# Other distances between moving rows and weights in four feed-forwards, and a later switch to normalized x in one

## The chip, the cores and the metric

The kernel runs on one core of a Trainium2 chip. The metric is device time in microseconds: the median of three timed runs. One further execution was taken with the hardware profiler; all views below are of that one.

## What is computed

Two blocks follow one another on 256 rows of 1024 columns, all in float32. The first block (reference `first_block`) has two layers. Each has a feed-forward, a mixer (a state-space scan in layer 0, pooling in layer 1) and a second feed-forward, each on a normalized and modulated input; layer 0 runs beside them a second stream, the context `h`. The second block is another mixer network; the change does not touch it.

```python
def swiglu(u, wg, wu, wd):
    return (jax.nn.silu(u @ wg) * (u @ wu)) @ wd
...
def modulate(x, g, shift, scale):
    return rmsnorm(x, g) * (1 + scale) + shift
...
        x = x + 0.5 * m[:, 8] * swiglu(modulate(x, norm_g[i, 2], m[:, 6], m[:, 7]),
                                       ffn_w_gate[i, 1], ffn_w_up[i, 1], ffn_w_down[i, 1])
```

Gate and up have 1024 x 2816 weights, down has 2816 x 1024. The modulation `m` is a product of `silu(c)` with `ada_w`.

## The kernel before

Everything is held transposed: columns on the 128 partitions, tokens along them, so x is 8 tiles of 128 x 256 (`xT`, `KD` = 8, `T` = 256). A product in float32 is made of three matmuls in float32r (`mm3`, L301 to L303): high weights by high rows, high weights by low rows, low weights by high rows. The weights stand still (128 x 128 a matmul), the rows move (256, 258 or 512 columns).

`Weights` streams all weights of the program in one order. `load` (L52) fetches a raw piece on SP's queue; `prepare` makes of 1024 columns the high part `whi` on ScalarE (L68) and the low part `wlo` on VectorE (L69), into rings of four buffers each, two units ahead of their use. A unit is one gate or up tile of eight 128 x 128 pieces, so 24 matmuls. A buffer of the ring is free once the unit four before has been used up.

There are four feed-forwards. The first in time is joint: latent and context rows together, 512 columns, in three parts, its intermediate in `hh0` and `hl0` (high and low). The other three are calls of `ffn` (L810), on the latent rows alone: the text calls them the first, second and third. Each goes over 22 tiles of the intermediate (`f`): gate into the bank `pg`, up into `pu`, SiLU, product, and a split into `hh` and `hl`; then eight down tiles of 66 matmuls each, into `po`.

The rows of the first five tiles (`FIRST`) are `xh` and `xl`, x scaled but without its reciprocal norm R and shift, with two columns more that hold the shift, so 258. Their results are scaled and shifted afterwards on VectorE and ScalarE (`shifted` L379, L828 to L833). Meanwhile `norm_mod` (L395) writes the normalized x into `xn` (high by ScalarE L398, low by VectorE L399, from a product at L397), two of its eight tiles after each of f = 1 to 4 (`EARLY`, L812, L839). From tile 5 on the rows are `xn`, 256 columns, and ScalarE and VectorE have one operation each in place of the six. From f = 2 on, the first and second feed-forward also make one modulation column a tile (`ada_column`, L236: 128 x 1024 on VectorE, its weights `adaraw` loaded on SP's queue). Five PSUM banks serve `pg`, `pu` and `po` in turn.

The order on each engine is set by a scheduling layer, from the order in which the program is written; engines work through it in order.

`lead` puts an unused tile of that many bytes ahead of `xn`, and so moves all tiles of the feed-forward. All buffers of `whi` and `wlo` start at 320 bytes modulo 512, and weight pieces step by 512 bytes, rows by 1024 or 2048. So within a stage the distance from weights to moving rows, modulo 512, is the same for all matmuls.

Of the kernel before, what the change touches and what calls it, by code (L numbers as in the profile page):

```python
# [10 lines left out]
F32 = mybir.dt.float32  # L11
F32R = mybir.dt.float32r
AF = mybir.ActivationFunctionType
# [4 lines left out]
P = 128  # L18
# [71 lines left out]
def build(ctx: ExitStack, tc, a, out):  # L90
# [22 lines left out]
    def nm(s):  # L113
        uid[0] += 1
        return f"{s}{uid[0]}"
# [173 lines left out]
    def half_cols(l, s, m):  # L289
        t = consts.tile([P, KD], F32, name=f"H{l}{s}{m}")  # L290
        V.tensor_scalar(t, mod(l, s, m), 0.5, None, op0=OP.mult)
        return t
# [514 lines left out]
                pass  # L807


    def ffn(R, nxt, H, tail, n_ada, late=None, lead=0):  # L810

        EARLY = ((), (0, 1), (2, 3), (4, 5), (6, 7))  # L812
        FIRST = len(EARLY)
        with tc.tile_pool(name=nm("ffn"), bufs=1) as fp:
            if lead:
                fp.tile([P, lead // 4], F32, name=nm("lead"))
            xn = [fp.tile([P, KD, T], F32R, name=nm("xn")) for _ in range(2)]
            hh = fp.tile([P, NF, T], F32R, name=nm("hh"))
            hl = fp.tile([P, NF, T], F32R, name=nm("hl"))
            for f in range(NF):  # L820
                pg, pu = bank("mm", nm("pg")), bank("mm", nm("pu"))

                (mh, ml), n = ((xh, xl), T + 2) if f < FIRST else (xn, T)
                dense_tile(pg[:, :n], W.next(), 0, KD, mh, ml, n)
                dense_tile(pu[:, :n], W.next(), 0, KD, mh, ml, n)
                tg = tmp.tile([P, T], F32, tag="t1k", name=nm("tg"), bufs=2)
                if f < FIRST:
                    tu = tmp.tile([P, T], F32, tag="t1k", name=nm("tu"), bufs=2)  # L828
                    shifted(pg, R, tg)
                    b = tmp.tile([P, 1], F32, tag="bg", name=nm("bg"), bufs=4)  # L830
                    V.tensor_copy(b, pu[:, T:T + 1])
                    V.tensor_mul(tu, pu[:, :T], R)
                    V.scalar_tensor_tensor(tu, tu, b, tg, op0=OP.add, op1=OP.mult)  # L833
                else:
                    tu = tg
                    S.activation(tg, pg[:, :T], AF.Silu)
                    V.tensor_mul(tu, pu[:, :T], tg)
                split(hh[:, f, :], hl[:, f, :], tu)
                for d in EARLY[f] if f < FIRST else ():  # L839
                    norm_mod(xn[0][:, d, :], xn[1][:, d, :], d, xT[:, d, :], R, nxt.A, nxt.B)  # L840
                if f == 2 and late:
                    late()
                if f > 1:
                    ada_do(n_ada)
            table()
            for d in range(KD):
                po = bank("mm", nm("po"))
                for f0, n in PARTS:
                    dense_tile(po[:, :T], W.next(), 0, n, hh, hl, T, f0, f0 == 0, f0 + n == NF)
                V.scalar_tensor_tensor(xT[:, d, :], po[:, :T], H[:, d:d + 1], xT[:, d, :],  # L850
                                       op0=OP.mult, op1=OP.add)
                tail(d)
# [76 lines left out]

    with l0_stack:  # L930
        with tc.tile_pool(name="ffn0", bufs=1) as fp:
            fp.tile([P, 32], F32, name="lead0")
            hh = fp.tile([P, 8, 2 * T], F32R, name="hh0")
            fp.tile([P, 40], F32, name="lead1")
            hl = fp.tile([P, 8, 2 * T], F32R, name="hl0")
            for f0, nf in PARTS:
                for f in range(nf):
                    pg, pu = bank("mm", nm("pg")), bank("mm", nm("pu"))
                    dense_tile(pg, W.next(), 0, KD, uh, ul, 2 * T)
                    dense_tile(pu, W.next(), 0, KD, uh, ul, 2 * T)  # L940
                    sg = fp.tile([P, 2 * T], F32, tag="sg", name=nm("sg"), bufs=2)
                    S.activation(sg, pg, AF.Silu)
                    V.tensor_mul(sg, sg, pu)
                    split(hh[:, f, :], hl[:, f, :], sg)
                    if f0 + f == 0:
                        for n, src in enumerate(("c", "c_ctx")):
                            cond_load(l0, n, a[src])
                            S.activation(csb[n], csb[n], AF.Silu)
                    ada_do(4)
                if f0 == 0:  # L950
                    ada_until(0, 2)
                    h2c, h2x = half_cols(0, 1, 2), half_cols(0, 0, 2)
                last = f0 + nf == NF
                if last:
                    ada_until(0, 4)
                    A1c, A1x = scale_cols(0, 1, 1, 4), scale_cols(0, 0, 1, 4)
                    B1c, B1x = mod(0, 1, 3), mod(0, 0, 3)
                    st2 = l0.tile([P, 2 * T], F32, name="st2")
                    shifts(B1x, T - 2)
                    table()  # L960
                for d in range(KD):
                    po = bank("mm", nm("po"))
                    dense_tile(po, W.next(), 0, nf, hh, hl, 2 * T)
                    V.scalar_tensor_tensor(xC[:, d, :], po[:, :T], h2c[:, d:d + 1], xC[:, d, :],
                                           op0=OP.mult, op1=OP.add)
                    V.scalar_tensor_tensor(xT[:, d, :], po[:, T:], h2x[:, d:d + 1], xT[:, d, :],
                                           op0=OP.mult, op1=OP.add)
                    if last:
                        sq = l0.tile([P, 2 * T], F32, tag="sq2", name=nm("sq2"), bufs=1) if d else st2
                        S.activation(sq[:, :T], xC[:, d, :], AF.Square)  # L970
                        S.activation(sq[:, T:], xT[:, d, :], AF.Square)
                        if d:
                            V.tensor_add(st2, st2, sq)
                        scaled(d, xT[:, d, :], A1x, T)
                    ada_do(3)
# [40 lines left out]
    with tc.tile_pool(name="ada1", bufs=1) as ap:  # L1016
        ada_state["pool"] = ap
        cond_load(ap, 0, a["c"])
        ada_stop(1, 8)
        ffn(R, nxt, H8, after_ffn1, 1, lambda: S.activation(csb[0], csb[0], AF.Silu), lead=320)  # L1020


        nxt = state["n"]
        R = nxt.st.rstd()

        def after_ffn2(d):
            if d == 0:
                state["n"] = Next(scale_cols(1, 0, 1, 4))
            state["n"](d)

        ffn(R, nxt, half_cols(1, 0, 2), after_ffn2, 1, lead=320)
        ada_until(1, 8)

    def pool_phase(pp, st, pmat, tail):
# [78 lines left out]
            state["n"] = Final()  # L1113
        state["n"](d)

    ffn(R, nxt, half_cols(1, 0, 8), after_ffn3, 0, lead=320)
    f = state["n"]

    def norm_first():
# [744 lines left out]
```

## Time and profile before

| | us |
|---|---|
| median of three timed runs | 1912.84 |
| the three runs | 1906.72, 1912.84, 1916.23 |
| the profiled execution | 1924.61 |
| its span | 1922.8 |
| mean granted clock of TensorE in it | 0.989 |

| stage | from | to |
|---|---|---|
| first feed-forward, tiles 0 to 4 | 726.84 | 757.83 |
| the same, tiles 5 to 21 | 757.83 | 862.18 |
| the same, down | 862.18 | 924.37 |
| second, tiles 0 to 4 | 924.37 | 954.09 |
| second, tiles 5 to 21 | 954.09 | 1050.70 |
| second, down | 1050.70 | 1112.88 |
| third, tiles 0 to 4 | 1128.59 | 1158.19 |
| third, tiles 5 to 21 | 1158.19 | 1251.57 |
| third, down | 1251.57 | 1311.41 |

The times of stages are starts of their first matmul in the profiled execution, from the start of its span. Matmuls overlap: one is listed with a duration of 276 ns or more, while the next starts after less than half of that. So a stage is read by its length and its number of matmuls, not by their durations. The granted clock is 1.00 at 2.4 GHz and 0.50 at 1.2 GHz.

### The profile page before, as it was taken

The page shows a single profiled execution, that of the slowest core. Times are in us where ns is not written, and L with a number is a line of the kernel's source. Part 1 is how long each engine was busy: PE and PEld are TensorE (multiplying, and loading weights), DVE is VectorE, ACT ScalarE, POOL GpSimd, SP SyncE. Part 2 cuts the span into 40 slices and gives each one's busy share as a digit, 9 for nine tenths or more (in the row PEclk, how much of TensorE's full clock was granted, in tenths as well). Part 3 has the DMA queues.
Part 4 walks back from the last instruction along what each step waited for, and adds up shares of the span by engine and source line. Part 5 has one row for each costly group of instructions (what it writes and reads, how often), then busy time and mean ns, then how long its engine had stood idle before and what let it go on. Part 6 is the DMA issues. An engine that isn't in the chain of part 4 may idle for free.

```text
span 1922.8 us, 37344 instructions
## 1 busy us (share of the span) xinstructions
PE 1869.3 (97%) x15576; PEld 1690.3 (88%) x15576; DVE 1425.4 (74%) x2539; ACT 1041.7 (54%) x1659; POOL 0.2 (0%) x4
## 2 busy tenths in 40 slices
PE   8999999998999999999999999999999999999998
PEld 3888888887767789999999999999998998999887
DVE  5898788777898799855755587566698765698764
ACT  5322222355778666544544455456556656756573
POOL 0000000000000000000000000000000000000000
PEclk9999999999999999999999999999999999999999
DMA  8767788633333437755555645556544254536232
GB/s 314 261 238 280 278 301 312 231 120 114 110 107 135 132 132 277 256 172 184 198 178 170 195 161 182 178 192 197 195 149 174 88 164 153 189 115 221 94 110 88
DMA packets 82441, 353.12 MB, mean 184 GB/s; under 512 B 12928, under 2 KB 31424, under 8 KB 51552
## 3 DMA queue, kind: packets, MB, share of 16 engines
q1 hardware_dynamic: 82272, 350.73, 52.5%
q8 instruction: 122, 2.00, 0.4%
q14 instruction: 47, 0.39, 0.1%
HBM read 348.80 MB, written 1.12 MB: 182 GB/s over the span
## 4 chain that ended last, share of the span: by engine, by line
PE 83%; ACT 6%; DVE 5%; DMA 3%; issue 2%; SPq 0%; DVEq 0%; ACTq 0%
PE po L301 6%; PE po L303 6%; PE po L302 6%; PE pg L301 5%; PE pg L302 5%; PE pg L303 5%; PE pu L302 5%; PE pu L303 5%; PE pu L301 5%; PE pfm L301 3%; PE pfm L302 3%; PE pfm L303 3%; ACT whi L68 2%; PE ptm L1202 1%; PE pw L302 1%
## 5 line engine op out<-in xcount | busy, mean ns | idle before, releaser
L68 ACT ACTIVATE whi<-wraw 128x1024 fp32r<-128x1024 f32 (+1 forms) x485 | 504.2, 1041 | 668.5 <-PE po L302 189.2
L69 DVE TENSOR_TENSOR wlo<-wraw,whi 128x1024 fp32r<-128x1024 f32 (+1 forms) x485 | 580.7, 1199 | 242.9 <-ACT whi L68 238.3
L301 PE MATMUL po<-hh,whi 128*128 128x256 f32 (+1 forms) x704 | 217.5, 309 | 0.0
L303 PE MATMUL po<-hh,wlo 128*128 128x256 f32 (+1 forms) x704 | 216.9, 308 | 0.0
L302 PE MATMUL po<-hl,whi 128*128 128x256 f32 (+1 forms) x704 | 216.6, 308 | 0.0
L236 DVE SCALAR_TENSOR_TENSOR adascr<-adaraw,csb 128x1024 f32<-128x1024 f32 x152 | 185.7, 1222 | 31.9 <-DMA adaraw<-in_ada 29.4
L301 PE MATMUL pfm<-xh,whi 128*128 128x256 f32 x640 | 190.2, 297 | 0.0
L302 PE MATMUL pfm<-xl,whi 128*128 128x256 f32 x640 | 182.4, 285 | 0.0
L303 PE MATMUL pfm<-xh,wlo 128*128 128x256 f32 x640 | 180.9, 283 | 0.0
L303 PEld LDWEIGHTS po<-hh,wlo 128*128 128x128 f32 x704 | 133.0, 189 | 8.2
L301 PEld LDWEIGHTS po<-hh,whi 128*128 128x128 f32 x704 | 132.9, 189 | 7.5
L302 PEld LDWEIGHTS po<-hl,whi 128*128 128x128 f32 x704 | 132.2, 188 | 7.8
L301 PEld LDWEIGHTS pfm<-xh,whi 128*128 128x128 f32 x640 | 122.8, 192 | 3.7 <-issue 1.4
L302 PEld LDWEIGHTS pfm<-xl,whi 128*128 128x128 f32 x640 | 122.6, 192 | 2.1 <-issue 1.4
L303 PEld LDWEIGHTS pfm<-xh,wlo 128*128 128x128 f32 x640 | 122.4, 191 | 1.2 <-issue 1.0
L301 PE MATMUL pg<-xn,whi 128*128 128x256 f32 x408 | 115.5, 283 | 2.8 <-ACT xn L398 1.6
L302 PE MATMUL pg<-xn,whi 128*128 128x256 f32 x408 | 115.5, 283 | 0.8 <-DVE xn L399 0.8
L301 PE MATMUL pu<-xn,whi 128*128 128x256 f32 x408 | 114.6, 281 | 0.7 <-ACT whi L68 0.7
L303 PE MATMUL pg<-xn,wlo 128*128 128x256 f32 x408 | 115.0, 282 | 0.0
L302 PE MATMUL pu<-xn,whi 128*128 128x256 f32 x408 | 114.6, 281 | 0.0
L303 PE MATMUL pu<-xn,wlo 128*128 128x256 f32 x408 | 114.5, 281 | 0.0
L301 PE MATMUL pg<-xh,whi 128*128 128x512 f32 (+1 forms) x296 | 104.1, 352 | 0.4 <-ACT xh L369 0.4
(468 smaller groups left out, 4814.7 us busy)
## 6 DMA issues: line engine op xcount, KB each, us to landing
wraw<-in_ffn_gu SPq DMA_DIRECT2D x88, 1024.0 KB, 5.0
adaraw<-in_ada SPq DMA_DIRECT2D x64, 1024.0 KB, 6.8
wraw<-in_w SPq DMA_DIRECT2D x60, 1024.0 KB, 5.0
wraw<-in_ffn_d SPq DMA_DIRECT2D x24, 960.0 KB, 4.8
wraw<-in_ssd_wi SPq DMA_DIRECT2D x20, 1024.0 KB, 5.1
wraw<-in_w_out SPq DMA_DIRECT2D x16, 1024.0 KB, 5.1
wraw<-in_ffn_d SPq DMA_DIRECT2D x24, 448.0 KB, 3.3
adan<-in_ada_n SPq DMA_DIRECT2D x8, 1024.0 KB, 8.3
```

The lines of the kernel that those rows point to most:

```text
L68: nc.scalar.activation(hi[:, :n], raw[:, o:o + n], AF.Copy)
L69: nc.vector.tensor_sub(lo[:, :n], raw[:, o:o + n], hi[:, :n].bitcast(F32))
L236: V.scalar_tensor_tensor(scr, t[:, h, :], 1.0, csb[s], op0=OP.mult, op1=OP.mult, accum_out=macc[l, s][:, n:n + 1])
L301: TE.matmul(o, wh, xh, start=start, stop=False)
L302: TE.matmul(o, wh, xl, start=False, stop=False)
L303: TE.matmul(o, wl, xh, start=False, stop=stop)
L1202: TE.matmul(o, h, wh[:, sl], start=k == 0, stop=False)
```

## The change

It changes two things. In the first feed-forward, `EARLY` writes one tile of `xn` after each of f = 1 to 8, so that `FIRST` is 9: tiles 5 to 8 use `xh` and `xl` with 258 columns too. And the unused tiles get other sizes, now with a second one between `xn` and `hh`, so that six distances change.

```diff
-    def ffn(R, nxt, H, tail, n_ada, late=None, lead=0):
-
-        EARLY = ((), (0, 1), (2, 3), (4, 5), (6, 7))
+    def ffn(R, nxt, H, tail, n_ada, late=None, lead=(0, 0), EARLY=((), (0, 1), (2, 3), (4, 5), (6, 7))):
...
-            if lead:
-                fp.tile([P, lead // 4], F32, name=nm("lead"))
+            if lead[0]:
+                fp.tile([P, lead[0] // 4], F32, name=nm("lead"))
             xn = [fp.tile([P, KD, T], F32R, name=nm("xn")) for _ in range(2)]
+            if lead[1]:
+                fp.tile([P, lead[1] // 4], F32, name=nm("lead"))
...
-            fp.tile([P, 32], F32, name="lead0")
+            fp.tile([P, 48], F32, name="lead0")
             hh = fp.tile([P, 8, 2 * T], F32R, name="hh0")
-            fp.tile([P, 40], F32, name="lead1")
+
...
-        ffn(R, nxt, H8, after_ffn1, 1, lambda: S.activation(csb[0], csb[0], AF.Silu), lead=320)
+        ffn(R, nxt, H8, after_ffn1, 1, lambda: S.activation(csb[0], csb[0], AF.Silu), lead=(192, 384),
+            EARLY=((),) + tuple((d,) for d in range(KD)))
...
-        ffn(R, nxt, half_cols(1, 0, 2), after_ffn2, 1, lead=320)
+        ffn(R, nxt, half_cols(1, 0, 2), after_ffn2, 1, lead=(160, 192))
...
-    ffn(R, nxt, half_cols(1, 0, 8), after_ffn3, 0, lead=320)
+    ffn(R, nxt, half_cols(1, 0, 8), after_ffn3, 0, lead=(224, 192))
```

As the two programs lay their tiles out, the distances from weights to moving rows, in bytes modulo 512:

| rows | before | after |
|---|---|---|
| joint, `hh0` and `hl0` | 0 and 160 | 64 and 64 |
| first, `xn` | 192 | 64 |
| first, `hh` and `hl` | 192 | 448 |
| second, `xn` | 192 | 32 |
| second, `hh` and `hl` | 192 | 224 |
| third, `xn` | 192 | 96 |
| third, `hh` and `hl` | 192 | 288 |

`xh` and `xl` stay at 192. The output projection before the first feed-forward, whose rows `gh` and `gl` stand at 128 and 384, is not changed.

The distances move no instruction; `EARLY` does. On VectorE, where the last rows of `xn` are written, the order before is (`adascr` is a modulation column, `nm` the product of x and R, `bg` a shift):

```order
L833 SCALAR_TENSOR_TENSOR tu_6950<-tu_6950,bg_6955,tg_6949 128x256
L377 TENSOR_TENSOR xl<-macc_89,xh 128x8x2
L397 SCALAR_TENSOR_TENSOR nm_6961<-xT,A_3048,rstd_6546 128x256
L308 TENSOR_TENSOR hl_6567<-tu_6950,hh_6566 128x256
L397 SCALAR_TENSOR_TENSOR nm_6965<-xT,A_3048,rstd_6546 128x256
L399 SCALAR_TENSOR_TENSOR xn_6565<-nm_6961,macc_87,xn_6564 128x256
L236 SCALAR_TENSOR_TENSOR adascr_7243,macc_89<-adaraw_7105,csb_6558 128x1024
L399 SCALAR_TENSOR_TENSOR xn_6565<-nm_6965,macc_87,xn_6564 128x256
L236 SCALAR_TENSOR_TENSOR adascr_7310,macc_89<-adaraw_7105,csb_6558 128x1024
L264 TENSOR_TENSOR macc_89<-macc_89,c_ada_b 128x8
L236 SCALAR_TENSOR_TENSOR adascr_7380,macc_89<-adaraw_7241,csb_6558 128x1024
L837 TENSOR_TENSOR tg_7033<-pu_6974,tg_7033 128x256
```

The place of the last `xn` in the changed program, four tiles later:

```order
L236 SCALAR_TENSOR_TENSOR adascr_7475,macc_89<-adaraw_7269,csb_6557 128x1024
L399 SCALAR_TENSOR_TENSOR xn_6564<-nm_7187,macc_87,xn_6563 128x256
L236 SCALAR_TENSOR_TENSOR adascr_7544,macc_89<-adaraw_7406,csb_6557 128x1024
L834 TENSOR_TENSOR tu_7254<-pu_7194,rstd_6545 128x256
L236 SCALAR_TENSOR_TENSOR adascr_7611,macc_89<-adaraw_7406,csb_6557 128x1024
L835 SCALAR_TENSOR_TENSOR tu_7254<-tu_7254,bg_7259,tg_7253 128x256
L377 TENSOR_TENSOR xl<-macc_89,xh 128x8x2
L286 SCALAR_TENSOR_TENSOR A_11090<-macc_89,c_norm_g 128x8
L397 SCALAR_TENSOR_TENSOR nm_7265<-xT,A_3047,rstd_6545 128x256
L308 TENSOR_TENSOR hl_6567<-tu_7254,hh_6566 128x256
L399 SCALAR_TENSOR_TENSOR xn_6564<-nm_7265,macc_87,xn_6563 128x256
L236 SCALAR_TENSOR_TENSOR adascr_7680,macc_89<-adaraw_7542,csb_6557 128x1024
```

In both, columns stand ahead of the last row of `xn`; it now follows the results of tile 8 (`tu_7254`), not of tile 4 (`tu_6950`), and one row is left after them in place of two.

On TensorE, where the rows `xn` that came late are first read (`pg_6973`, `pu_6974`, `pg_7040` are gate and up of tile 5 and gate of tile 6), the order before has, after 36 matmuls with the four rows written first:

```order
L302 MATMUL pg_7040<-xn_6565,whi_6975 128x256
L303 MATMUL pg_7040<-xn_6564,wlo_6976 128x256
L301 MATMUL pg_6973<-xn_6564,whi_6891 128x256
L301 MATMUL pu_6974<-xn_6564,whi_6919 128x256
L301 MATMUL pg_7040<-xn_6564,whi_6975 128x256
L302 MATMUL pg_6973<-xn_6565,whi_6891 128x256
L303 MATMUL pg_6973<-xn_6564,wlo_6892 128x256
```

The changed program starts with `xn` at gate of tile 9 (`pg_7273`, then `pu_7274`, `pg_7340`, `pu_7341`). The first read of the seventh row stands after 46 matmuls, that of the eighth, here from the third line on, after 84:

```order
L302 MATMUL pu_7341<-xn_6564,whi_7303 128x256
L303 MATMUL pu_7341<-xn_6563,wlo_7304 128x256
L301 MATMUL pg_7273<-xn_6563,whi_7195 128x256
L301 MATMUL pu_7274<-xn_6563,whi_7223 128x256
L301 MATMUL pg_7340<-xn_6563,whi_7275 128x256
L301 MATMUL pu_7341<-xn_6563,whi_7303 128x256
L302 MATMUL pg_7273<-xn_6564,whi_7195 128x256
```

So before, TensorE goes back to tile 5 for a row after 36 matmuls, and again for the last two; now it goes back to tile 9 after 46 and, for the last, after 84.

## Rows read from the trace of the kernel before

**Rows 1.** The page of the profiled execution: busy time of each engine.
```profile
PE 1869.3 (97%) x15576; PEld 1690.3 (88%) x15576; DVE 1425.4 (74%) x2539; ACT 1041.7 (54%) x1659; POOL 0.2 (0%) x4
```

**Rows 2.** Busy times by stretch: start:end, us, then PE, PEld, DVE, ACT, POOL, clock, DMA.
```profile
726.84:757.83 30.99, 30.46 (x245) 29.61 (x244) 29.92 (x63) 20.89 (x33) 0.00 (x0) 1.00 0.91 331
757.83:785.86 28.03, 24.04 (x170) 23.03 (x169) 25.15 (x47) 12.30 (x21) 0.00 (x0) 0.88 0.71 254
785.86:862.18 76.32, 76.32 (x650) 76.32 (x649) 50.98 (x72) 37.55 (x55) 0.00 (x0) 1.00 0.58 204
862.18:924.37 62.19, 62.19 (x531) 62.19 (x529) 36.48 (x46) 30.46 (x40) 0.00 (x0) 1.00 0.59 196
954.09:960.24 6.15, 5.94 (x50) 5.74 (x49) 5.07 (x13) 3.39 (x7) 0.00 (x0) 1.00 0.51 179
960.24:1050.70 90.46, 90.46 (x771) 90.46 (x769) 52.15 (x65) 43.91 (x66) 0.00 (x0) 1.00 0.51 174
1167.25:1251.57 84.32, 84.32 (x746) 84.32 (x745) 51.67 (x65) 42.90 (x65) 0.00 (x0) 1.00 0.53 185
```

**Rows 3.** Timeline, DVE, first feed-forward: start, us, line, operation.
```profile
747.08 0.87 DVE L397 SCALAR_TENSOR_TENSOR nm<-xT,A,rstd 128x256 f32<-128x256 f32 x2
...
754.17 1.22 DVE L69 TENSOR_TENSOR wlo<-wraw,whi 128x1024 fp32r<-128x1024 f32 x1
755.30 0.48 DVE L399 SCALAR_TENSOR_TENSOR xn<-nm,macc,xn 128x256 fp32r<-128x256 f32 x1
755.70 0.48 DVE L397 SCALAR_TENSOR_TENSOR nm<-xT,A,rstd 128x256 f32<-128x256 f32 x1
756.10 0.42 DVE L383 TENSOR_TENSOR tg<-pg,rstd 128x256 f32<-128x256 f32 x1
...
756.49 1.22 DVE L236 SCALAR_TENSOR_TENSOR adascr<-adaraw,csb 128x1024 f32<-128x1024 f32 x1
```

**Rows 4.** Timeline, PE, same place; in brackets the idle time before and its releaser.
```profile
763.65 0.39 PE L301 MATMUL pg<-xn,whi 128*128 128x256 f32 x1 [1.42 <-ACT xn L398]
...
765.05 0.39 PE L302 MATMUL pg<-xn,whi 128*128 128x256 f32 x1 [0.78 <-DVE xn L399]
...
767.19 0.41 PE L302 MATMUL pg<-xn,whi 128*128 128x256 f32 x1
767.40 0.41 PE L303 MATMUL pg<-xn,wlo 128*128 128x256 f32 x1
...
776.21 0.54 PE L301 MATMUL pg<-xn,whi 128*128 128x256 f32 x1 [0.72 <-ACT whi L68]
```

**Rows 5.** Timeline, DVE, the end of the normalized x.
```profile
759.57 1.22 DVE L69 TENSOR_TENSOR wlo<-wraw,whi 128x1024 fp32r<-128x1024 f32 x1
...
764.51 0.88 DVE L399 SCALAR_TENSOR_TENSOR xn<-nm,macc,xn 128x256 fp32r<-128x256 f32 x2
...
770.98 0.48 DVE L399 SCALAR_TENSOR_TENSOR xn<-nm,macc,xn 128x256 fp32r<-128x256 f32 x1
...
774.49 2.35 DVE L69 TENSOR_TENSOR wlo<-wraw,whi 128x1024 fp32r<-128x1024 f32 x2
```

**Rows 6.** Busy times by stretch, after the first waits of rows 4.
```profile
766.00:770.00 4.00, 4.00 (x24) 4.00 (x23) 3.55 (x10) 1.76 (x4) 0.00 (x0) 0.57 0.91 336
```

**Rows 7.** Busy times by stretch, tiles 3 and 4, rows of 258 columns.
```profile
746.23:757.83 11.60, 11.60 (x99) 11.60 (x98) 11.58 (x26) 7.39 (x11) 0.00 (x0) 1.00 0.88 311
```

**Rows 8.** Groups by line, PE, 1710.6 to 1712.9, then 1714.9 to 1717.3.
```profile
L302 PE MATMUL pfm<-xl,whi 128*128 128x256 f32 x7 | 1.9, 276 | 0.0
...
L302 PE MATMUL pfm<-xl,whi 128*128 128x256 f32 x7 | 2.0, 282 | 0.0
```

**Rows 9.** Busy times by stretch, end of the output projection before the feed-forward.
```profile
718.90:726.84 7.94, 7.94 (x69) 7.94 (x68) 6.91 (x17) 6.80 (x13) 0.00 (x0) 1.00 0.26 108
```

**Rows 10.** Busy times by stretch, joint feed-forward: gate and up, then down.
```profile
60.00:120.00 60.00, 60.00 (x259) 48.44 (x258) 59.11 (x96) 17.02 (x21) 0.00 (x0) 1.00 0.65 232
130.43:175.03 44.60, 44.60 (x194) 36.04 (x193) 39.63 (x68) 9.12 (x10) 0.00 (x0) 1.00 0.75 264
```

## The prediction

> **What bounds the kernel.** The page comes first: TensorE (PE) is busy for 97% of the span and no other engine for more than 74% [rows 1]. In the feed-forwards this means matmul behind matmul, so a stage costs its number of matmuls times the spacing of their starts, plus the places where PE waits. Two questions follow: what sets the spacing, and where are the waits.
>
> For the spacing I cut the span at stage borders and divided. From 785.86 to 862.18, 27 gate or up tiles of 24 matmuls start: 76.32 / 648 = 117.8 ns. The down projection of the same feed-forward gives 62.19 / 528 = 117.8, the second feed-forward's gate and up 90.46 / 768 = 117.8. In the third it is 84.32 / 744 = 113.3 [rows 2]. (The counts in the rows take in two or three matmuls that were still running at the border.) Shapes, clock and distances between rows and weights are the same in all three, so 256 columns have a wide and a close spacing, and the distance alone doesn't choose. In the last block the same matmul, with its distance kept, is 276 ns long in one run of tiles and 282 in another, 4 us later [rows 8]: after an interruption PE falls into one or the other, and keeps it until the next.
>
> For the waits I read the stretch where tile 5 of the first feed-forward takes over from tile 4, since there the rows switch from xh to xn. Seven tiles, 168 matmuls, take 28.03 us against 168 x 117.8 = 19.8: 8.2 us lost. The same place in the second feed-forward takes 6.15 us for 48 matmuls, 0.5 lost [rows 2]. In the first, PE waits 1.42 and 0.78 us for the normalized x (xn) [rows 4]; then the granted clock drops, to a mean of 0.57 over 4 us [rows 6], the lower level being 1.2 GHz, and starts are 0.21 apart [rows 4]: some 18 matmuls, 1.7 us. This first group costs about 4.0. Next come three waits for split weights like the 0.72 at 776.21 [rows 4], with a second fall of the clock: the remaining 4.2.
>
> Both come from VectorE (DVE), which is busy for 29.92 of the first 30.99 us [rows 2]. It works in order, and between the split at 759.57 and the next at 774.49 it makes no low parts of weights at all [rows 5].
>
> **The later switch.** DVE's price for one tile, as starts follow one another: a weight split 1.13, a scalar-tensor-tensor 0.40 [rows 3], a plain one 0.34 and a modulation column 1.14 (each followed 0.08 before its listed end, as the split is). Tiles 2 to 4 now: two splits 2.26, scaling and bias 1.21, hl 0.34, column 1.14, two rows of xn at 0.80 each: 6.6 us, against PE's 11.60 / 2 = 5.80 [rows 7]. DVE falls behind by 0.8 a tile. With one row a tile it needs 5.8, as much as PE: it falls behind no further, but catches up no more either.
>
> The last row of xn decides. From 747.08 [rows 3], where both programs stand alike, the changed DVE order has 13 splits, 11 columns, 22 scalar-tensor-tensors, 21 plain and 16 small ones (0.08 each) up to it: 14.7 + 12.5 + 8.8 + 7.1 + 1.3 = 44.4 us, so it starts at 791.5. PE begins tile 9 at 757.83 + 4 x 5.80 = 781.0 and has 84 matmuls, 9.9 us, before it needs that row, where before it had 36 (4.2 us). ScalarE's half of the row is ready at about 791.7: a wait of 0.8, and the first group's clock loss goes. The second group stays, because the order after it is unchanged in kind: the next split starts at about 794.5, while PE has used up tiles 9 and 10 by 781.0 + 96 x 0.1178 + 0.8 = 793.1. So 8.2 becomes 0.8 + 4.2 = 5.0. Against that, 4 x 48 matmuls have 258 columns, at 11.60 / 96 = 120.8 [rows 7] in place of 117.8: +0.6. **Together -2.6.** The bounds: if the place becomes as good as in the second feed-forward, -7.7 + 0.6 = -7.1; if DVE, now without any slack for nine tiles, loses 0.8 a tile over the four added ones, +3.2 - 2.6 = +0.6. What else moves has cover: the modulation columns stay the same in number, three of SP's loads change places with their neighbours on a queue whose DMA engines are 0.58 busy after the switch, and ScalarE, which writes the high half of xn, is busy for 20.89 of the first 30.99 us [rows 2].
>
> **The distances.** They add no instruction and no wait; only the spacing can change. For 256 columns the rows bound it: 113.3 below, and above it the output projection at distances 128 and 384, 7.94 / 67 = 118.5 [rows 9]. What each place could gain or lose:
> - first, 624 + 528 = 1152 matmuls of 256 columns, now wide: -5.1 at the close spacing, +0.8 at 118.5. Its new distances, 64 and 448, are like 192 modulo 128, so I take 0.
> - second, 48 + 768 + 528 = 1344, now wide: -6.0 to +0.9. Third, 1344, now close: 0 to +7.0. Both go to distances that are 32 or 96 modulo 128. The only such row now is hl of the joint down projection, at 160: its stretch runs at 44.60 / 192 = 232.3 ns, while 192 gives 60.00 / 257 = 233.5 [rows 10]. It leans to the close side, so I take close for both: -6.0 and 0.
> - joint down, 528 of 512 columns, goes to 64, like 192 modulo 128: 528 x 1.2 ns = +0.6. As bounds I take the same step either way.
>
> The Trainium skill (SBUF — State Buffer, Who interferes with whom) states that TensorE reads moving rows and weights through two ports of their own and never waits on another engine; by that, distances change nothing, and the sum would be the switch alone. The two spacings at one distance agree with it as far as they go; 118.5 at another distance, never 113.3, does not settle it.
>
> **Sum.** -2.6 - 6.0 + 0.6 = -8.0 us on the profiled execution's 1924.6 (span 1922.8). That execution is 11.8 above the median of 1912.84, and the three timed runs lie 9.5 apart: about the size of two feed-forwards at the wide spacing (5.1 to 7.0 each). So the timed runs may already have close stretches where the profile shows wide ones. I carry the sum over to the median: **1904.8 us**, 0.42% less, just inside the 0.5% that a measurement of this kernel can tell from no change.
>
> **Rivals.**
> 1. Distances do nothing: the spacing of a run is set by how it starts [rows 8]. Only the switch counts: 1912.8 - 2.6 = 1910.2. Chance 0.24. (The rule of the Trainium skill's page SBUF — State Buffer comes to the same.)
> 2. The new distances hold the close spacing wherever it can be had: the first gains 5.1 as well, and with its early waits gone up to the whole -7.1: -13.1 to -17.6, 1895 to 1900. For it: every place would need only what the third already shows. Against: 64 modulo 128 has had both. Chance 0.27.
> 3. Slower: the third leaves the close spacing, as the output projection never has it [rows 9]: +7.0, with +0.9 and +0.8 in the others and +0.6 in the joint one: +9.3, less 2.6 or plus 0.6. That is 1919.5 to 1922.7. It decides if the third turns wide and the second does not turn close. Chance 0.16; half of it passes 0.5%.
>
> That leaves 0.33 for the forecast. It reaches over the 0.5% in about a quarter of its cases. Faster by more than 0.5%: 0.27 + 0.08 = 0.35. Slower by more: 0.08. Within: 0.57. The range, 1894 to 1919, holds rivals 1 and 2 all but their far ends, and the better edge of 3.
>
> **What would show it.** In the changed profile, tile 5 follows tile 4 without a wait; the switch comes after tile 8 with one wait for xn under 1 us, and the waits for weights and one fall of the clock stay; DVE still has a hole of about 11 us without a split. The second feed-forward's 768 gate and up matmuls take 87.0 us and its down projection 59.8; the third stays at 113.3. I am wrong if the spacing of a changed stage is below 113.3 or above 118.5, if the waits for weights go too, or if PE waits for DVE in tiles 2 to 8.

## The result, and the profile after

The change makes the kernel slower: 1925.4 us (1922.84 to 1928.52, six runs) against 1911.12 (six runs beside them), a ratio of 1.0066 with the interval 1.0042 to 1.009. Forecast were 1904.8 us and a range up to 1919. The forecast was wrong, in direction as well as in size.

The profiled executions hide this. That of the change took 1925.8 us, only 1.2 more than the 1924.6 of the profile before. So the first thing to explain is not a stage but why the two profiles agree where the medians are 14 us apart. Page of the change, busy times:

```profile
PE 1870.0 (97%) x15576; PEld 1693.4 (88%) x15576; DVE 1429.2 (74%) x2555; ACT 1042.1 (54%) x1659; POOL 0.2 (0%) x4
```

The totals are those of [rows 1]. By stretch there is a difference, and the signs are mixed. The change, busy times by stretch (start:end, us, then PE, PEld, DVE, ACT, POOL, clock, DMA): joint down; tiles 0 to 8 of the first feed-forward; the 168 matmuls behind them; its down projection; then tiles 6 to 21 and the down projection of the second, and the same of the third.

```profile
130.28:174.23 43.95, 43.95 (x193) 36.05 (x192) 39.32 (x68) 9.13 (x10) 0.00 (x0) 1.00 0.74 267
...
723.55:777.75 54.20, 53.65 (x436) 52.82 (x435) 53.11 (x108) 32.74 (x50) 0.00 (x0) 1.00 0.87 315
777.75:806.06 28.31, 23.94 (x170) 22.89 (x169) 22.98 (x45) 11.79 (x20) 0.00 (x0) 0.88 0.66 235
859.77:921.96 62.19, 62.19 (x531) 62.19 (x530) 36.49 (x46) 30.46 (x40) 0.00 (x0) 1.00 0.60 196
957.83:1047.43 89.60, 89.60 (x770) 89.60 (x769) 52.18 (x65) 43.96 (x66) 0.00 (x0) 1.00 0.51 176
1047.43:1109.91 62.48, 62.48 (x530) 62.48 (x529) 36.49 (x46) 30.49 (x40) 0.00 (x0) 1.00 0.60 196
1161.38:1253.64 92.26, 92.26 (x770) 92.25 (x769) 52.87 (x68) 44.65 (x67) 0.00 (x0) 1.00 0.50 171
1253.64:1315.25 61.61, 61.61 (x531) 61.61 (x530) 38.51 (x52) 33.30 (x47) 0.00 (x0) 1.00 0.61 198
```

Divided by 192, 528 or 768 matmuls these are spacings. **Joint down** went from 232.3 ns [rows 10] to 43.95 / 192 = 228.9. **First:** the down projection still has 117.8. **Second:** 89.60 / 768 = 116.7 for x at distance 32 and 62.48 / 528 = 118.3 for hidden at 224, where both had 117.8 [rows 2]. **Third:** 92.26 / 768 = 120.1 for x at 96 (120.0 without its few short waits) and 116.7 for hidden at 288, where 113.3 stood. From its first to its last matmul the third takes 189.6 us in place of 182.8.

**The switch.** The 168 matmuls behind the change of rows took 28.03 us and now take 28.31 [rows 2]: 28.31 - 168 x 0.1178 = 8.5 us lost, where 8.2 had been. PE's waits there have other causes, though. The change, what PE waited for from 755 to 812 (us in total, times, longest):

```profile
PE pg L303 <- DVE wlo L69: 1.9, 1, 1.9
PE pg L301 <- ACT whi L68: 1.0, 2, 0.7
PE pu L301 <- ACT whi L68: 0.7, 1, 0.7
PE pg L301 <- ACT xn L398: 0.7, 1, 0.7
```

Only 0.7 us is left of the waits for xn, in place of the 1.42 and 0.78 of [rows 4]. But PE now waits 1.9 for the low parts of weights. DVE's timeline in the change shows why:

```profile
788.59 0.48 DVE L399 SCALAR_TENSOR_TENSOR xn<-nm,macc,xn 128x256 fp32r<-128x256 f32 x1 [0.23 <-ACT xn L398]
791.48 1.22 DVE L236 SCALAR_TENSOR_TENSOR adascr<-adaraw,csb 128x1024 f32<-128x1024 f32 x1 [2.40 <-DMA adaraw<-in_ada]
...
792.75 1.22 DVE L236 SCALAR_TENSOR_TENSOR adascr<-adaraw,csb 128x1024 f32<-128x1024 f32 x1
...
794.23 2.35 DVE L69 TENSOR_TENSOR wlo<-wraw,whi 128x1024 fp32r<-128x1024 f32 x2
```

The last row of xn is written at 788.59, and next in DVE's order stand two modulation columns whose load has not landed. DVE stands still for 2.40 us, and the weight split queued behind the columns starts only at 794.23, 16.5 us after PE's first matmul of tile 9 (777.75). Then the clock falls, as before. The change, busy times by stretch:

```profile
791.00:795.00 4.00, 1.16 (x6) 0.59 (x4) 3.48 (x6) 2.69 (x5) 0.00 (x0) 0.96 0.25 104
795.00:800.00 5.00, 4.50 (x21) 4.50 (x22) 4.86 (x7) 1.13 (x2) 0.00 (x0) 0.50 0.47 154
```

The granted clock is 0.50, the 1.2 GHz level, after PE had been busy for only 1.16 of the 4 us before.

### The profile page after: what moved, and what is told of

Its sections match the earlier page's. It is cut to its first block, busy times and chain, and to the rows that moved or that the text cites. A ratio compares the mean times of both kernels' runs of the same rounds, so it can differ in the third digit from the quotient of the medians.

```text
span 1924.0 us, 37367 instructions
## 1 busy us (share of the span) xinstructions
PE 1870.0 (97%) x15576; PEld 1693.4 (88%) x15576; DVE 1429.2 (74%) x2555; ACT 1042.1 (54%) x1659; POOL 0.2 (0%) x4
## 4 chain that ended last, share of the span: by engine, by line
PE 84%; DVE 5%; ACT 5%; DMA 3%; issue 1%; SPq 0%; DVEq 0%; ACTq 0%
PE po L301 6%; PE po L303 6%; PE po L302 6%; PE pg L303 5%; PE pg L301 5%; PE pg L302 5%; PE pu L303 5%; PE pu L302 5%; PE pu L301 5%; PE pfm L301 3%; PE pfm L302 3%; PE pfm L303 3%; PE ptm L1205 2%; PE ptm L1206 2%; PE ptm L1207 2%; PE pw L301 1%
## 5 line engine op out<-in xcount | busy, mean ns | idle before, releaser
L301 PE MATMUL pg<-xh,whi 128*128 128x512 f32 (+1 forms) x328 | 113.0, 345 | 0.4 <-ACT xh L369 0.4
L302 PE MATMUL pg<-xl,whi 128*128 128x512 f32 (+1 forms) x328 | 113.0, 345 | 0.0
L303 PE MATMUL pg<-xh,wlo 128*128 128x512 f32 (+1 forms) x328 | 112.8, 344 | 0.1
L303 PE MATMUL pu<-xh,wlo 128*128 128x512 f32 (+1 forms) x328 | 112.8, 344 | 0.1
L301 PE MATMUL pu<-xh,whi 128*128 128x512 f32 (+1 forms) x328 | 112.7, 344 | 0.0
L302 PE MATMUL pu<-xl,whi 128*128 128x512 f32 (+1 forms) x328 | 112.7, 344 | 0.0
L301 PE MATMUL pg<-xn,whi 128*128 128x256 f32 x376 | 106.8, 285 | 1.9 <-ACT whi L68 1.0
```

What stands on the lines that cost most here:

```text
L301: TE.matmul(o, wh, xh, start=start, stop=False)
L302: TE.matmul(o, wh, xl, start=False, stop=False)
L303: TE.matmul(o, wl, xh, start=False, stop=stop)
```

## The experiments

All distances below are as in the part on the change: where the moving rows stand past the weights, modulo 512 bytes. "Lost at the switch" is always the time of the first 168 matmuls with rows of xn in the first feed-forward, less 168 times their spacing.

### 1. The kernel before, again

No edit.

> The kernel before, unchanged. Theory 1 (two spacings at distance 192): matmuls on 256 columns whose rows stand 192 bytes past the weights (mod 512) run at either 113.3 or 117.8 ns from start to start, which of them is drawn anew after each interruption, and the profiled execution before had drawn the wide one in the first and second feed-forward. So this profile can show another mixture: a feed-forward stage at 113.3 that stood at 117.8 before. The time is then some 1911 us, with runs apart by up to 10 us, and a profiled run with the first and second feed-forward close would stand near 1924.6 - 11 = 1913. Theory 2 (spacing is fixed by the place in the program): the first and second feed-forward show 117.8 and the third 113.3 again, as before; then the 14 us between the medians of the two kernels are not to be found in the spacing. Ratio 1.000 under both.

1913.49 us (12 runs), ratio 0.9986 (0.9965 to 1.0008); the runs of before beside it spread from 1907.38 to 1932.2. Its profiled execution took 1918.4 us. Busy times by stretch: down projection of the first, tiles 6 to 21 and down of the second, the same of the third.

```profile
859.43:919.27 59.84, 59.84 (x531) 59.84 (x530) 36.41 (x46) 30.52 (x40) 0.00 (x0) 1.00 0.61 202
955.16:1042.20 87.04, 87.04 (x771) 87.04 (x769) 52.15 (x65) 43.90 (x66) 0.00 (x0) 1.00 0.53 181
1042.20:1102.04 59.84, 59.84 (x531) 59.84 (x529) 36.41 (x46) 30.52 (x40) 0.00 (x0) 1.00 0.61 202
1153.50:1244.09 90.59, 90.59 (x770) 90.58 (x769) 52.85 (x68) 44.64 (x67) 0.00 (x0) 1.00 0.50 174
1244.09:1306.27 62.18, 62.18 (x530) 62.18 (x529) 38.50 (x52) 33.28 (x47) 0.00 (x0) 1.00 0.60 197
```

The same program shows the reverse of [rows 2]: the first and second feed-forward at 59.84 / 528 = 113.3 and the third at 117.8. So at 192 the spacing is drawn anew in each execution, and the place does not decide. The theory of a fixed place falls. One feed-forward takes 182.8 us close and 188.5 wide.

### 2. The switch alone

```
+        ffn(R, nxt, H8, after_ffn1, 1, lambda: S.activation(csb[0], csb[0], AF.Silu), lead=(320, 0),
+            EARLY=((),) + tuple((d,) for d in range(KD)))
```

> Only the later switch (normalized x behind eight tiles, not four, in the first feed-forward); all distances as before. Theory 1 (the distances made the change slower): the loss around the switch is as large as before (8.4 against 8.5 us in the two profiles), plus 0.6 us for 258 columns instead of 256: same as before within 1 us, ratio 0.9995 to 1.0008. Rival (the switch made it slower, by changing where the first and second feed-forward start again and with it which spacing they take): 1920 to 1927, ratio 1.005 to 1.008. My prediction's own term was -2.6 us, ratio 0.9986.

1916.14 us, ratio 1.0008 (0.9983 to 1.0034): no difference. In its profile 5.2 us are lost at the switch, DVE does not wait for the columns' load, and the clock falls for a shorter time (0.93 over the 168 matmuls, 0.88 in the change). Busy times of these 168 matmuls, then DVE's timeline from the last row of xn to the next split, which here starts 14.0 us after tile 9:

```profile
778.87:803.87 25.00, 22.38 (x170) 21.54 (x169) 22.90 (x45) 11.69 (x20) 0.00 (x0) 0.93 0.73 266
...
789.71 0.48 DVE L399 SCALAR_TENSOR_TENSOR xn<-nm,macc,xn 128x256 fp32r<-128x256 f32 x1 [0.23 <-ACT xn L398]
790.11 1.22 DVE L236 SCALAR_TENSOR_TENSOR adascr<-adaraw,csb 128x1024 f32<-128x1024 f32 x1
...
792.86 2.35 DVE L69 TENSOR_TENSOR wlo<-wraw,whi 128x1024 fp32r<-128x1024 f32 x2
```

### 3. The feed-forwards' distances alone

```
-        ffn(R, nxt, H8, after_ffn1, 1, lambda: S.activation(csb[0], csb[0], AF.Silu), lead=320)
+        ffn(R, nxt, H8, after_ffn1, 1, lambda: S.activation(csb[0], csb[0], AF.Silu), lead=(192, 384))
...
+        ffn(R, nxt, half_cols(1, 0, 2), after_ffn2, 1, lead=(160, 192))
...
+    ffn(R, nxt, half_cols(1, 0, 8), after_ffn3, 0, lead=(224, 192))
```

> Only the three feed-forwards' distances (64 and 448, 32 and 224, 96 and 288 in place of 192); switch and joint feed-forward as before. Theory 1 (none of the new distances has the close spacing of 113.3 ns; 192 has it in most executions of each stage): the first stays at 117.8, the second at 116.7 and 118.3, the third at 119.9 and 116.7, and the time is 1911 + 15 to 17 = 1926 to 1928, ratio 1.008 to 1.009. Rival (the spacing hangs on how a stage starts, not on the distance): same as before within 3 us, with one of these six stretches at 113.3.

1927.98 us (1925.59 to 1932.83), ratio 1.0063 (1.0043 to 1.0083). The spacings are those of the change: 117.8 and 117.8, 116.7 and 118.3, 120.0 and 116.7. This part holds the whole loss, as far as the times can tell. Busy times by stretch, tiles 6 to 21 and down of the second, the same of the third:

```profile
958.35:1047.95 89.60, 89.60 (x771) 89.60 (x770) 52.12 (x65) 43.92 (x66) 0.00 (x0) 1.00 0.51 175
1047.95:1110.43 62.48, 62.48 (x531) 62.48 (x530) 36.48 (x46) 30.49 (x40) 0.00 (x0) 1.00 0.59 196
1161.76:1254.03 92.27, 92.27 (x771) 92.26 (x769) 52.85 (x68) 44.67 (x67) 0.00 (x0) 1.00 0.50 171
1254.03:1315.62 61.59, 61.59 (x530) 61.59 (x529) 38.51 (x52) 33.30 (x47) 0.00 (x0) 1.00 0.60 198
```

### 4. The joint feed-forward alone

```
-            fp.tile([P, 32], F32, name="lead0")
+            fp.tile([P, 48], F32, name="lead0")
...
-            fp.tile([P, 40], F32, name="lead1")
```

> Only the joint feed-forward's down product at 64 and 64 in place of 0 and 160 (512 columns). Theory 1: its spacing goes from 232.3 to 228.9 ns in 192 rows of eight... worked out over its 528 matmuls 528 x 3.4 ns = -1.8 us, ratio 0.9990, and everything behind it as before. Rival (the time at which it ends shifts which spacing the later stages take): any time between 1905 and 1922, with the difference in the feed-forwards behind it and not in the joint one.

1916.31 us, ratio 0.9995 (0.9975 to 1.0015). The times can't tell 1.8 us from nothing. The profile has 228.9 ns per matmul in the first and third part of the down projection, as in the change. The second part has 235.6 on average, because PE waits once there for the low rows (`hl`) from DVE, 0.8 us, near its start; its other matmuls stand 229.0 apart.

### 5 and 6. The change again, and the change without its switch

Experiment 5 has no edit. Experiment 6, against the change:

```
-            EARLY=((),) + tuple((d,) for d in range(KD)))
```

> The change as it is, once more, beside its own parts on the same chip. Theory 1 (none of its distances has two spacings): its profile shows 117.8 and 117.8, 116.7 and 118.3, 119.9 and 116.7 ns in the three feed-forwards again, and its runs lie within some 8 us of each other, where those of the kernel before spread over 25 us. Rival (each start draws one of two spacings at every distance): one of the six stretches is at another spacing than in the first profile of the change.

> The change without the later switch: all new distances, the joint feed-forward's too, and x written behind four tiles as before. With no stage that can take two spacings, this shows what the switch is worth to within 1 us or so. My prediction: the switch gives 2.6 us, so this kernel takes 2.6 us more than the change. Rival (the profile of the change is typical: its waits for x went, but a wait of DVE for the modulation columns and half a clock came instead): no difference, within 1 us.

The change: 1928.67 us (1923.36 to 1933.63), 1.0067 (1.0047 to 1.0087). Without the switch: 1926.54 (1923.56 to 1933.49), 1.0056 (1.0036 to 1.0075). With runs that lie within some 10 us of each other the switch shows no gain. Lost at the switch were 6.8 us with it and 10.2 without it in these two profiles.

In one point the theory of single spacings fell. In the second profile of the change hidden at 448 (first) runs at 113.3, and x at 32 (second) at 90.45 / 768 = 117.8:

```profile
858.89:918.74 59.85, 59.85 (x531) 59.85 (x529) 36.42 (x46) 30.51 (x40) 0.00 (x0) 1.00 0.62 204
...
954.64:1045.09 90.45, 90.45 (x770) 90.45 (x769) 52.15 (x65) 43.87 (x66) 0.00 (x0) 1.00 0.51 174
```

So 448 has the close spacing too, and 32 has two, 116.7 and 117.8. It is the third that never left 120.0 and 116.7.

### 7 and 8. Other distances, other places

As in experiment 3, with other pairs. Experiment 7:

```
+        ffn(R, nxt, H8, after_ffn1, 1, lambda: S.activation(csb[0], csb[0], AF.Silu), lead=(128, 160))
...
+        ffn(R, nxt, half_cols(1, 0, 2), after_ffn2, 1, lead=(384, 96))
...
+    ffn(R, nxt, half_cols(1, 0, 8), after_ffn3, 0, lead=(32, 64))
```

Experiment 8:

```
+        ffn(R, nxt, H8, after_ffn1, 1, lambda: S.activation(csb[0], csb[0], AF.Silu), lead=(224, 192))
...
+        ffn(R, nxt, half_cols(1, 0, 2), after_ffn2, 1, lead=(448, 320))
...
+    ffn(R, nxt, half_cols(1, 0, 8), after_ffn3, 0, lead=(192, 384))
```

> Distances alone, six others: 0 and 160 in the first feed-forward, 256 and 352 in the second, 416 and 480 in the third; switch and joint feed-forward as before. Theory 1 (every distance but 192 has one spacing, 116.7 ns or more): all six between 116.6 and 120, time 1924 to 1932, ratio 1.004 to 1.009, runs within 8 us of each other. Rival (some distance has the close spacing, 113.3 ns, and it alone): a stretch at 113.3, which would be worth 816 x 3.4 = 2.8 us (x) or 528 x 3.4 = 1.8 us (hidden) below its neighbours.

> Distances alone, moved to other places: 96 and 288 (which the third had in the change) in the first feed-forward, 320 and 128 in the second, 64 and 448 (which the first had) in the third. Theory 1 (the spacing belongs to the distance, not to the place): 119.9 and 116.7 in the first, 117.8 and 117.8 in the third, one value between 116.6 and 120 each in the second. Rival (it belongs to the place, to what runs beside it on the other engines and the DMA queue): the first keeps 117.8 and 117.8, the third 119.9 and 116.7, whatever its distances.

Experiment 7: 1932.97 us, 1.0082 (1.0061 to 1.0103). Spacings: 120.0 at 0 and 117.3 at 160; 120.0 at 256 and at 352; 117.3 at 416 and 118.3 at 480. None is close.

Experiment 8: 1928.51 us, 1.0063 (1.0041 to 1.0084). 96 and 288 have 120.0 and 116.7 in the first as well, and 320 and 128 have 117.8 and 118.7: the spacing goes with the distance, not with the place. In the third, x at 64 has 117.8 and hidden at 448, behind it without a break, 113.3. Busy times by stretch, tiles 6 to 21 and down of the third:

```profile
1164.96:1255.55 90.59, 90.59 (x769) 90.57 (x769) 52.87 (x68) 44.67 (x67) 0.00 (x0) 1.00 0.50 174
1255.55:1315.40 59.85, 59.85 (x531) 59.85 (x529) 38.44 (x52) 33.33 (x47) 0.00 (x0) 1.00 0.61 203
```

### 9. Second and third back at 192

Against the change:

```
-        ffn(R, nxt, half_cols(1, 0, 2), after_ffn2, 1, lead=(160, 192))
+        ffn(R, nxt, half_cols(1, 0, 2), after_ffn2, 1, lead=(320, 0))
...
-    ffn(R, nxt, half_cols(1, 0, 8), after_ffn3, 0, lead=(224, 192))
+    ffn(R, nxt, half_cols(1, 0, 8), after_ffn3, 0, lead=(320, 0))
```

> The change with the second and third feed-forward put back to 192; the later switch, 64 and 448 in the first and 64 and 64 in the joint feed-forward stay. Theory 1 (the whole loss is in the second and third, which can no longer run at 113.3 ns): the time is that of the kernel before within some 3 us (ratio 0.998 to 1.0015), its runs spread over 10 us and more again, and the profile shows 113.3 or 117.8 throughout each of the two. Rival (the first feed-forward pays a part too, since x at 64 never takes 113.3): ratio 1.002 to 1.003, 1919 to 1923 us.

1917.37 us (1910.77 to 1930.22), ratio 1.0003 (0.9981 to 1.0025). Two stages put back, and the slowdown is gone; the spread is back as well, 19 us in place of 10. The profiled run took the slowest time of all, 1930.22, and had all three feed-forwards wide.

### 10. Modulation columns behind tile 11

Against the change; the zero taken from tile 11 holds back the columns, and leaves their values as they are.

```
-                if f == 2 and late:
-                    late()
-                if f > 1:
-                    ada_do(n_ada)
+                if f == 12 and late:
+                    z = tmp.tile([P, 1], F32, tag="bg", name=nm("z"), bufs=4)
+                    V.tensor_scalar(z, hl[:, 11, :1].bitcast(F32), 0.0, None, op0=OP.mult)
+                    late(z)
+                if f > 12:
+                    ada_do(2 * n_ada)
...
+        ffn(R, nxt, H8, after_ffn1, 1, lambda z: S.activation(csb[0], csb[0], AF.Silu, bias=z), lead=(192, 384),
```

> The change with the 16 modulation columns of the first feed-forward behind tile 11 instead of in tiles 2 to 11 (they depend there on a zero taken from tile 11), so that DVE has neither them nor their loads before it writes x and splits weights around the switch. Theory (the switch gained nothing because these columns, 1.22 us each, hold up DVE and stand ahead of the weights in the DMA queue): the first feed-forward loses under 4 us around the switch where the change lost 8.5 and 6.8, and the time is 3 to 5 us below the change's (1928.7 on the last chip), ratio to before 1.004 to 1.0055. Rival (the loss is PE's wait for the next weights' own split and the clock behind it): the loss stays 5 to 8.5 us and the time the change's.

1920.9 us, ratio 1.0024 (1.0004 to 1.0043). Busy times by stretch: tiles 0 to 8, then the 168 matmuls behind them.

```profile
723.05:777.25 54.20, 53.66 (x437) 52.82 (x436) 49.04 (x100) 33.38 (x53) 0.00 (x0) 1.00 0.71 258
777.25:797.40 20.15, 20.10 (x171) 19.90 (x169) 12.93 (x21) 10.30 (x16) 0.00 (x0) 1.00 0.47 170
```

20.15 us in place of 28.31, the clock at 1.00 throughout, no wait of PE for weights or xn: 0.4 us lost. The loss was the columns' work on DVE and their loads.

### 11. A candidate

Against experiment 10; the joint feed-forward stays at 64 and 64.

```
-        ffn(R, nxt, H8, after_ffn1, 1, lambda z: S.activation(csb[0], csb[0], AF.Silu, bias=z), lead=(192, 384),
+        ffn(R, nxt, H8, after_ffn1, 1, lambda z: S.activation(csb[0], csb[0], AF.Silu, bias=z), lead=(320, 0),
...
+        ffn(R, nxt, half_cols(1, 0, 2), after_ffn2, 1, lead=(320, 0))
...
+    ffn(R, nxt, half_cols(1, 0, 8), after_ffn3, 0, lead=(320, 0))
```

> A version that might beat both: all feed-forwards at 192, joint feed-forward at 64 and 64, the later switch, and the modulation columns behind tile 11. Theory: -1.8 us of the joint feed-forward and -3 to -5 us around the switch against the kernel before: 1909 to 1912, ratio 0.9965 to 0.998. Rival (neither the switch nor the columns matter): -1.8 us, ratio 0.999.

1907.4 us (1903.37 to 1923.63), ratio 0.9961 (0.9935 to 0.9986): faster than both kernels. 0.5 us lost at the switch in the profile, and all three feed-forwards close in that execution, which took 1904.2.

### 12. Two distances in one stage

As in experiment 3, with these leads:

```
+        ffn(R, nxt, H8, after_ffn1, 1, lambda: S.activation(csb[0], csb[0], AF.Silu), lead=(320, 384))
...
+        ffn(R, nxt, half_cols(1, 0, 2), after_ffn2, 1, lead=(64, 128))
...
+    ffn(R, nxt, half_cols(1, 0, 8), after_ffn3, 0, lead=(320, 128))
```

> Distances alone: x at 192 and hidden at 64 in the first feed-forward, 448 and 64 in the second, 192 and 320 in the third. Theory 1 (a stage draws one of two states at its start and keeps it; 192 and 448 show it as 113.3 or 117.8; 64 and 320 have 117.8 in either): where x stands at 113.3, hidden goes to 117.8 at once. Rival (64 and 320 have both spacings too, and were only drawn wide so far): hidden stays at the spacing of x in each of the three, 113.3 among them.

One run, 1921.99 us. Busy times by stretch, second feed-forward (x at 448, hidden at 64), then third (192 and 320):

```profile
958.34:1045.38 87.04, 87.04 (x770) 87.04 (x769) 52.15 (x65) 43.89 (x66) 0.00 (x0) 1.00 0.53 181
1045.38:1107.57 62.19, 62.19 (x530) 62.19 (x529) 36.47 (x46) 30.50 (x40) 0.00 (x0) 1.00 0.59 197
1159.04:1246.27 87.23, 87.23 (x770) 87.22 (x769) 52.84 (x68) 44.66 (x67) 0.00 (x0) 1.00 0.52 181
1246.27:1308.45 62.18, 62.18 (x530) 62.18 (x529) 38.50 (x52) 33.29 (x47) 0.00 (x0) 1.00 0.60 197
```

In one unbroken run of matmuls, x runs at 113.3 and hidden at 117.8, so a new spacing needs no interruption. Where x and hidden both stand at 192, they had the same spacing in all 20 stages profiled here. So distance and drawn state set the spacing together.

### 13 to 15. What the switch itself is worth

Experiment 13 is experiment 10 without the switch, 14 is experiment 10 again beside it, 15 is the candidate without the switch; the edit is that of experiment 6.

> The change with the modulation columns behind tile 11, and x written behind four tiles as before the change: columns moved, no switch. Theory (the switch pays once DVE has room: x of eight rows still needs 8 x 0.96 us of DVE beside the weights' splits before tile 5): some 3 to 5 us are lost around the switch, so 2.5 to 4.5 us more than with both. Rival (the columns alone were the loss): under 1 us lost, and the time 0.6 us below that with both, since 192 matmuls fewer are on 258 columns.

> Columns behind tile 11 and the later switch once more, beside the kernel without the switch: 0.4 us lost around the switch as on the other chip, ratio to before 1.0024 within its interval.

> The candidate (192 in all feed-forwards, 64 and 64 in the joint one, columns behind tile 11) without the later switch. If the switch pays: ratio 0.997 to 0.9985. If the columns alone were the loss: 0.995 to 0.9965, as the candidate with it (0.9961).

Columns moved, no switch: 1918.86 us, 1.0019 (0.9996 to 1.0042). Columns moved and switch: 1919.55, 1.0033 (1.0015 to 1.0051). Candidate without the switch: 1910.14, 0.9977 (0.9955 to 0.9998), an interval that overlaps that of the candidate with it. Experiment 13, the 168 matmuls behind tile 4:

```profile
757.78:778.11 20.33, 20.33 (x171) 20.03 (x170) 15.34 (x27) 11.38 (x19) 0.00 (x0) 1.00 0.49 173
```

0.5 us lost without the switch, 0.4 and 0.5 with it (experiments 10 and 14). With the columns out of the way the old place of the switch is as good in the profiles; my theory that 3 to 5 us would be lost there falls. The times alone don't decide it: the ratio of experiment 15 lies in the range set for a switch that pays, that of 13 on the other side of 14, and in both pairs the intervals overlap.

Experiment 14 brought a surprise in the first feed-forward: x stood at 64, which had 117.8 in all ten other stages, and ran at 113.3; hidden at 448 behind it ran at 117.8, the reverse of experiment 8. Busy times by stretch, tiles 10 to 21, then down:

```profile
785.02:850.30 65.28, 65.28 (x578) 65.28 (x577) 53.78 (x82) 32.33 (x48) 0.00 (x0) 1.00 0.75 268
850.30:912.49 62.19, 62.19 (x530) 62.19 (x529) 39.90 (x54) 32.47 (x44) 0.00 (x0) 1.00 0.62 204
```

## Why the prediction was wrong

**The baseline.** "I carry the sum over to the median" is the step that failed first. The text itself noted that the timed runs may already have close stretches where the profile shows wide ones, and then took -6.0 us for turning one of them close. Over the profiles here, the feed-forward stages at 192 were close in 13 of 22. The profile before was a bad draw, 13.5 us above the median of its kernel's six runs. Two wide stages of three explain some 4 us of that (11.1 us above three close ones, where 9 wide in 22 would make 7.0 on average, an estimate); the rest is not traced. A gain that most executions already have can't be had again.

**The distances, second and third: -6.0 and 0.** The step "It leans to the close side, so I take close for both" failed. It rested on one average of 232.3 against 233.5 at 512 columns [rows 10]. Measured: 116.7 and 118.3, 120.0 and 116.7, and no profile shows 113.3 there. The upper bound of 118.5 failed as well, by the 120.0. At 192 in seven profiles the second and third together took 370.5 us on average (365.4 to 377.1); in the change they take 188.0 + 189.6 = 377.6: 7.1 us more. The third rival had this mechanism and the price of the third (+7.0; measured 189.6 - 182.8 = 6.8). It priced the first and second from their wide stretches (+0.8 and +0.9), but added its sum to a median whose runs hold close ones, and so ended at 1919.5 to 1922.7. The range stopped at 1919, below both, though the text says that it holds the better edge. The runs confirm the cause: distances alone 1.0063, second and third put back 1.0003.

**The distances, first: 0.** 64 and 448 were close in 1 of 11 and 3 of 10 stages, 192 in 4 of 7 in the first feed-forward. At 5.1 us for its 1152 matmuls that is some 2 us more on average, an estimate from few draws. Together with the 7.1 above that makes 9 us of the 12 (8 to 16) that distances alone cost; the rest is within the interval.

**The joint feed-forward: +0.6.** Wrong in sign. "64, like 192 modulo 128" gave 228.9 ns, not 233.5: 1.7 us less over the three parts (122.7 to 121.0 us). The bounds, 0.6 either way, were too narrow for it.

**The switch: -2.6.** The wait for xn came out as forecast: one, 0.7 us (forecast 0.8), DVE busy for 53.11 of the 54.20 us of tiles 0 to 8, no wait for DVE in them, +0.6 us for 258 columns. The step that failed is "The second group stays", with "the next split starts at about 794.5", 13.5 us after tile 9. The order there is indeed unchanged in kind: in both programs two columns stand between the last row of xn and the next split. But the sum has no wait of DVE for the columns' load. It was 2.40 us in the change (0.6 in all before), so the split came 16.5 us after tile 9, PE waited 1.9 us for it, and the clock fell behind that. In experiment 2, where DVE did not wait, the split came after 14.0 us and 5.2 us were lost, near the forecast's 13.5 and 5.0: the step holds in that execution and not in the others. Of the four profiles with the switch and the columns at their old tiles, three have this wait, 2.0 to 2.4 us; why the load lands so late is not shown. The 8.2 that the sum started from was one draw too: the eight such profiles without the switch lost 5.3 to 10.2 us, 7.9 on average, the four with it 5.2 to 8.5, 7.2 on average. A gain of 0.7, less 0.6 for 258 columns, is nothing. The text counted the columns as the same in number and asked what they cost DVE (1.14 each), but not what stands behind each in DVE's order while it waits. Moving them (experiment 10) takes the loss away, about 7 us by the times (1.0067 and 1.0066 to 1.0024 and 1.0033, each to within some 0.002), and beside that no gain of the switch shows (experiments 13 to 15). Whether it was the columns' work on DVE or their loads was not taken apart.

**The rule weighed there.** By the Trainium skill (SBUF — State Buffer, Who interferes with whom), the moving rows and the weights have independent ports and contention comes from one port pair of other engines only; rival 1 took it to mean that distances do nothing. The trace does not agree with that use of it: at 256 columns x has 120.0 ns at 96 in the third feed-forward and in the first (experiment 8), where at 192 it has 113.3 or 117.8, all at a granted clock of 1.00.

**What stays open.** What draws the state is not shown. That 64 and 448 in one run gave wide and wide, wide and close, and close and wide needs at least three states, if a state holds for the run. Which of them a timed run had can't be seen without its profile. The weights start at the same place modulo 512 in every kernel here, so the runs do not tell the distance from the rows' own address. And the account above falls short for the whole change: 7.1 and 2 us more, 1.7 less and nothing for the switch make some 7 of its 13 us (1.0066 and 1.0067), a little below both intervals (8 to 17 and 9 to 17).

## What to carry to other kernels

Before a term is taken from a profile, ask whether the profiled execution is a typical one: a profile 12 us above the median of its kernel, or runs that spread by 25 us, can mean that stages have more than one speed, and a second profile of the same program can tell which. Price an edit of addresses only by rows at those very addresses, and against the mixture that the old ones give. And where an engine works in order, look at what stands behind an instruction that waits for a load: moving work that no matmul waited for, the modulation columns, gave about 7 us, and moving the work that PE did wait for gave nothing.

## What was unexpected in the hardware

- The spacing of matmuls on 256 columns depends on where the moving rows stand past the weights modulo 512 bytes (or on the rows' address alone, see above): 113.3 or 117.8 ns at 64, 192 and 448, 117.8 at 320, 116.7 or 117.8 at 32, 116.7 at 288, 117.3 at 160 and 416, 118.3 at 224 and 480, 118.7 at 128, 120.0 at 0, 96, 256 and 352. Distances 256 apart share a value in all seven pairs measured.
- With 512 columns the same program drew 232.3 and 231.1 ns at 0 and 160 in different executions; 64 and 64 gave 228.9 in all ten profiles, apart from single waits.
- With the same three kinds of waits at the switch, the clock fell in the profiles of the kernel before and of experiment 1 (0.88 over the 168 matmuls), and stayed at 1.00 in that of experiment 4, where 5.5 us were lost in place of 8.2. Its busy times over these matmuls:

```profile
755.91:781.19 25.28, 21.17 (x171) 20.07 (x169) 24.89 (x47) 12.31 (x21) 0.00 (x0) 1.00 0.76 271
```
